# A list scheduler's price for matmuls, changed from one pair of constants to another

## The chip, the cores and the metric
One core of a Trainium2 chip. Its engines (TensorE for products, VectorE and ScalarE for elementwise work, SyncE for issuing transfers) each run their own queue of instructions in program order and wait for each other through semaphores. The metric is the device time of one execution, in microseconds.

## What is computed
A trunk of two layers over 256 latent tokens and 256 context tokens of width 1024. Each layer is: a SwiGLU sub-layer (width 2816), a mixer sub-layer, and a second SwiGLU sub-layer.

```
x = layer_norm(alpha*x + 0.5*gate * (silu(h@wg) * (h@wu)) @ wd)   # h = x*(1+scale)+shift
u,k,v,q,z,b,c,g = split(h @ w_in)
y_a = S5(u)           # two directions, state carried from context to latent
y_b = attention(q,k,v)   # 8 heads; latent: 4x64 neighbourhood + all context
y_c = b * conv3(c*z)
m   = sum_i sigmoid(g_i) * (y_i @ w_branch_i)
x   = layer_norm(alpha*x + gate * (m @ w_out))
x   = second SwiGLU sub-layer, as the first
```

Shift, scale and gate of every sub-layer come from products of a conditioning vector with `w_mod` (adaLN). In the last layer the context is needed only up to the mixer's keys, values and S5 states, so most work from there on has 256 columns in place of 512.

## The kernel before
Activations lie with features on the partitions and tokens along the free axis, in 8 tiles of 128 x 512 (context 0 to 255, latent 256 to 511). Every factor of a product is split into two parts of a rounded type (`hi`, and `lo` for what the rounding left out), and `mm3` issues three products, hi·hi, hi·lo and lo·hi, in place of one fp32 product. A few products of S5 and of the statistics are in plain fp32.

Weights come block by block (128 x 1024 fp32) through three raw buffers. ScalarE makes `whi` (`rounder`, L426), VectorE makes `wlo` (`remainder`, L453), both into a ring of three places, and TensorE gives a place back when a block's products are done (`release`, L485). A SwiGLU sub-layer takes 22 pairs of blocks `wg`, `wu` (`ffn`, L760), with 8 x 3 products each, and then the `wd` blocks (`residual`, L797), whose last tile goes stream by stream, so that one stream's LayerNorm (`normalize`, L647) can run under the other's products. `entry_products` (L737) are the next phase's first four products, feature tile by feature tile as they are normalized. The mixer (L1347) runs the S5 batches (L1147), attention units (`attend`, L1274) and the convolution beside its projections. Work that needs no activation runs beside it all: the dot products of adaLN on VectorE (`mod_chunks`, L519) and the S5 tables (`s5_tables`, L953).

The order of all this is not written out. Each line of work is a generator that names, ahead of each instruction, its engine and operands. The class `Plan` (L59) keeps a clock for each engine and a ready time for each tile. `run` (L106) takes the line whose next instruction can start first by these clocks; among those within 0.08 us it takes the one of better priority; `op` (L74) then books the instruction's cost:

```
end = max([self.t[eng], self.now] + [self.at(i) for i in ins]) + cost
self.ready[o.tensor.name] = end + self.LATENCY[eng]
```

The priorities (L222) run from statistics over LayerNorm, evacuation, the weight stream, attention, S5 and late work down to the main line of products (`P_MAIN`), which comes last. Room in the pools, banks of PSUM and places of the ring are counted in the same clock. VectorE's cost is 0.07 + columns/960 us (L284) and ScalarE's 0.09 + columns/1200, with additions for extra operands (L328). TensorE's is booked in `mm` (L349).

Of the kernel before, what the change touches and what calls it, by code (L numbers as in the profile page):

```python
# [9 lines left out]
F32R = mybir.dt.float32r  # L10
# [16 lines left out]
NORM_ACT = (True, False)  # L27
# the order of the mixers' heads, two by two, and channels of the convolution
ORDERS = ("h0 h1 c0 h2 c1 c2 h3 c3", "h0 h1 c0 h2 c1 c2 h3 c3")
# [8 lines left out]
N_SHIFT = 2  # L38
# whether the two parts of the values share a pass, by layer
SIDE = (True, False)  # L40
# [18 lines left out]
class Plan:  # L59
    """Engines run their instructions in program order. The lines of work are generators that say, ahead of each  # L60
    instruction, its engine and its operands (or what else they wait for); the one whose instruction can start first,
    by a rough count of the engines' time, puts it into that order."""

# [75 lines left out]
class Room:  # L139
    """a count of the tiles of a pool: lines of work wait until there is room for theirs"""  # L140

# [3 lines left out]
    def take(self, n, late=False):  # L145
        """what can come late leaves the kept part to the others"""
        def room():
            return self.n >= n + late * self.kept
        if not room():
            yield "WAIT", room  # L150
        self.n -= n
# [5 lines left out]
class Shift:  # L157
    """a tile that holds the columns of the later stream only"""

# [8 lines left out]
class Block:  # L168
    """a block of weights, split; for a product of k parts"""

# [4 lines left out]
def block_order():  # L175
# [10 lines left out]
    for l in range(DEPTH):  # L186
# [20 lines left out]
        ffn(l, 1)  # L207
    # the first blocks of a phase, which do not wait for the ring, come earlier than they are needed
    starts = [i for i, k in enumerate(order) if i and (k[0] == "wg" and k[3] == 0 or k[0] == "in" and k[2] == 0)]
# [10 lines left out]

# the order in which lines of work take an engine that several could have
P_STAT, P_CHAIN, P_ENTRY, P_NORM, P_EVAC, P_SOON, P_STREAM, P_ATT, P_S5, P_LATE, P_MAIN = range(11)  # L222


def _build(ctx, tc, nc, A):
# [50 lines left out]
    def pair(name, sl):  # L276
        """the two parts of a factor of the tensor engine: rounded, and what that left out"""
        if sl.start == 0:
            return slot(name + "hi", dt=F32R), slot(name + "lo", dt=F32R)
        t = slot(name, (128, 2, 256), F32R)  # L280
        return Shift(t[:, 0], 256), Shift(t[:, 1], 256)

# [1 line left out]
    def dve(o, ins, rate=1.0, extra=()):  # L284
# [64 lines left out]
    def mm(o, l, r, start, stop):  # L349
        PE.matmul(o, l, r, start=start, stop=stop)  # L350
        n = _free(r)
        P.op("PE", max(0.1077, n * 0.000421) if r.dtype == F32R else max(0.215, n * 0.00168), [o], (l, r))

# [20 lines left out]

# [1 line left out]
    order = block_order()  # L376
# [28 lines left out]
    def nth(key):  # L405
        """which of a phase's first blocks it is"""
        if key[0] in ("wg", "wu"):
            return 2 * key[3] + (key[0] == "wu")
        return key[2] if key[0] == "in" else len(order)

    def place(key):
        """where the two parts of a block go: a phase's first ones wait for its start beside the ring"""
        if key[0] in ("wg", "wu") and key[1:3] == (0, 0):
            return "slot" if nth(key) < N_FIRST else "ring"
        return "big" if nth(key) < 3 else "ring"
# [76 lines left out]

# [1 line left out]
    cT = const("cT", [128, KT, 2])  # L494
# [11 lines left out]

# [1 line left out]
    modt, vecs, gates = {}, {}, {}  # L508

    def mod_rows():  # L510
        """silu of the two conditioning vectors, on every partition"""
        rows = []
        for s in range(2):
            rows.append(big("crow"))
            yield from dma_(rows[s], A["crow"][s])
            yield from act_(rows[s], rows[s], AF.Silu)
        return rows
# [30 lines left out]
    def mod_vectors(l, i, sh, sc, lm, streams):  # L548
        """scale and shift of the modulated LayerNorm: t -> t*A + B"""
        yield from wait(lambda: (lm, sh) in modt and (lm, sc) in modt)  # L550
# [35 lines left out]

# [1 line left out]
    class Norm:  # L588
# [7 lines left out]
        def evac(self, m, ps, streams):  # L596
            """add a tile of the sub-layer's output"""
            key = (self.l, self.i)
# [16 lines left out]
        def shift(self):  # L615
            """a mean of the first tiles, so that the sums of squares stay near the variance"""
            sl = self.sl
# [29 lines left out]
        def normalize(self, s, done):  # L647
            """the statistics of a stream, token by token on the partitions, and back; then tile by tile"""
            yield from wait(lambda: self.late[s] == KT - N_SHIFT)
# [17 lines left out]
            give_bank(p)  # L667
            # minus the guarded variance; then Newton's steps for its root's inverse, each times a power of two
            for _, _, de, nv, *_ in groups:
# [67 lines left out]
    def entry_products(keys, streams):  # L737
        """the first four products of a phase, k by k as the modulated stream arrives"""
        pss = yield from bank_set("en", len(keys))
# [16 lines left out]

# [1 line left out]
    filled = [0]  # L758
# [38 lines left out]
    def residual(l, i, streams, key, cuts, src, n_tail, tail):  # L797
        """the products of a sub-layer's end, the sum with the residual and its LayerNorm; then the next phase's
        first products. The last blocks go stream by stream, so that one stream's LayerNorm runs under the other's"""
        sl = span(streams)  # L800
# [38 lines left out]

# [1 line left out]
    NS = 32 * DEPTH  # L841
# [9 lines left out]
    def cmul_(o0, o1, a0, a1, b0, b1, t, neg=False):  # L851
        """(o0, o1) = a*b, or its real part and minus its imaginary one"""
        yield from vtt_(o0, a0, b0, OP.mult)
        yield from vtt_(t, a1, b1, OP.mult)
        yield from vtt_(o0, o0, t, OP.subtract)
        yield from vtt_(o1, a0, b1, OP.mult)
        yield from vtt_(t, a1, b0, OP.mult)
        if neg:
            yield from stt_(o1, o1, -1.0, t, OP.mult, OP.subtract)
        else:  # L860
            yield from vtt_(o1, o1, t, OP.add)

    def s5_pre():
        """lam_bar, its phasor and decay over a chunk and the factor of b, per state"""
        yield from SL.take(4)
# [87 lines left out]
    def s5_tables(l):  # L953
        """what of S5 does not depend on its input, for the mixer to load: the powers of lam_bar over a chunk with b and
        with c, the kernel within a chunk, and the phasors"""
        yield from wait(lambda: l in SP)
# [65 lines left out]
    def rc_piece(rc, r, c):  # L1022
        """the readout of a state column: five powers of 32 channels"""
        n = 4 * r + c
        return rc[n // 3][:, 160 * (n % 3):160 * (n % 3) + 160]
# [88 lines left out]
    def s5(l, U, GH, G5, streams):  # L1114
        """the batches of two pairs of groups: states of the chunks, their scan in a rotating frame, readout"""
        sp = SP[l]
# [104 lines left out]
        def readout(b, M, rc, L):  # L1221
# [28 lines left out]
            g = YT[m].rearrange("p c i -> p (c i)")  # L1250
            # gelu as x sigmoid(2 sqrt(2 / pi) (x + 0.044715 x^3)), the same as its form with tanh
            yield from SL.take(1)
# [19 lines left out]

# [1 line left out]
    def attend(h, s, kq, Vt, y, bias, loading, next_bias, side):  # L1274
        """one head of one stream"""
        khi, klo, qhi, qlo = kq
# [52 lines left out]
        for kt in range(n):  # L1329
            hi, lo = pt[kt // 2]  # L1330
            v = Vt[kt][h // 4][:, h % 4]
            yield "PE", [hi, lo, v] + ([o] if kt == 0 else [])
            # side by side, the two parts of the values take one pass, and a sum when their product is copied
            if side:
# [10 lines left out]

# [1 line left out]
    def mixer(l, streams, N, ready, tail):  # L1347
# [25 lines left out]
        def chunks(m, ps):  # L1373
            """channels and the steps of a chunk on the partitions, chunks along the free axis"""
            yield from SL.take(1)
# [245 lines left out]

# [1 line left out]
    def first_products():  # L1623
        """the adaLN vectors of the first sub-layer, feature tile by feature tile, shared between the tensor engine
        and the vector engine, and the first products behind them"""
        mod0 = const("mod0_0", [128, KT, 2])
# [244 lines left out]
```

## Time and profile before

| | us |
|---|---|
| runs | 2198.79, 2201.69, 2203.39 |
| median | 2201.69 |
| profiled execution, span | 2202.1 |
| TensorE busy | 2151.3 (98%) |
| VectorE busy | 1669.5 (76%) |
| ScalarE busy | 1040.0 (47%) |
| DMA | 363.32 MB, mean 165 GB/s |

The page gives no other time of the profiled execution than its span. Busy time counts an engine as busy from an instruction's start to its end; products overlap, so the spacing of their starts, not the length of one, tells what a stream of them takes. The granted clock (PEclk) is the share of TensorE's full 2.4 GHz.

### The profile page before, as it was taken

Reading aid. Unit: us, or ns where it says so; the run is one execution under the profiler, and the core shown is the slowest. Engines: PE = TensorE matmul, PEld = TensorE weight load, DVE = VectorE, ACT = ScalarE, POOL = GpSimd, SP = SyncE. Lnnn points to the kernel's source line nnn. Section 1 sums busy time; section 2 is a strip of 40 time slices with the busy share of each in tenths; the row PEclk is TensorE's granted clock in tenths of the full one; section 3 lists DMA queues with packets and bytes.
Section 4 is the critical chain, followed back from the end, with each engine's and each line's share of the span. In section 5 each row is a group of like instructions: output and inputs, shape, how many; then the busy total and the mean of one; then the engine's idle time right before and its main releaser. Section 6 shows DMA issues by size and latency. Waiting matters only on the chain.

```text
span 2202.1 us, 32955 instructions
## 1 busy us (share of the span) xinstructions
PE 2151.3 (98%) x12090; PEld 1866.1 (85%) x12090; DVE 1669.5 (76%) x3987; ACT 1040.0 (47%) x1938; POOL 0.2 (0%) x4
## 2 busy tenths in 40 slices
PE   8999999999999999999999999999999999998997
PEld 5888888878888888988888898888888889998997
DVE  7799986887888856889838779973448988776555
ACT  5332225766654354632222585542226556555443
POOL 0000000000000000000000000000000000000000
PEclk9999999999999999999999999999999999998998
DMA  7666645353334333177624537862334544554553
GB/s 287 209 215 213 216 139 173 116 196 115 116 126 154 97 142 126 69 250 240 196 91 135 172 112 258 292 225 93 102 112 154 166 154 151 184 178 146 183 174 123
DMA packets 131970, 363.32 MB, mean 165 GB/s; under 512 B 15968, under 2 KB 41952, under 8 KB 131808
## 3 DMA queue, kind: packets, MB, share of 16 engines
q1 hardware_dynamic: 131808, 361.21, 48.8%
q8 instruction: 95, 1.56, 0.3%
q14 instruction: 67, 0.55, 0.1%
HBM read 331.79 MB, written 29.36 MB: 164 GB/s over the span
## 4 chain that ended last, share of the span: by engine, by line
PE 90%; DVE 5%; ACT 2%; DMA 1%; issue 1%; SPq 0%; ACTq 0%; DVEq 0%
PE psd L350 21%; PE pswu L350 17%; PE pswg L350 17%; PE pg L350 8%; PE en L350 7%; PE pbr L350 4%; PE pk L350 2%; PE pz L350 2%; PE Y L350 1%; PE pq L350 1%; PE pb L350 1%; PE pc L350 1%; PE sc L350 1%; PE pvv L350 1%; PE v L350 1%; DVE wlo L288 1%
## 5 line engine op out<-in xcount | busy, mean ns | idle before, releaser
L329 ACT ACTIVATE whi<-raw 128x1024 fp32r<-128x1024 f32 (+2 forms) x427 | 421.3, 988 | 885.1 <-issue 339.7
L288 DVE TENSOR_TENSOR wlo<-raw,whi 128x1024 fp32r<-128x1024 f32 (+2 forms) x427 | 483.3, 1133 | 285.7 <-ACT whi L329 278.2
L350 PE MATMUL psd<-ghi,whi 128*128 128x512 f32 (+1 forms) x594 | 221.8, 373 | 0.0
L350 PE MATMUL psd<-ghi,wlo 128*128 128x512 f32 (+1 forms) x594 | 217.4, 366 | 0.0
L350 PE MATMUL psd<-glo,whi 128*128 128x512 f32 (+1 forms) x594 | 217.3, 366 | 0.0
L350 PE MATMUL pswu<-hhi,whi 128*128 128x512 f32 x472 | 185.8, 394 | 0.0
L350 PE MATMUL pswg<-hhi,whi 128*128 128x512 f32 x472 | 185.2, 392 | 0.0
L350 PE MATMUL pswu<-hhi,wlo 128*128 128x512 f32 x472 | 183.9, 390 | 0.0
L350 PE MATMUL pswu<-hlo,whi 128*128 128x512 f32 x472 | 183.8, 389 | 0.0
L350 PE MATMUL pswg<-hhi,wlo 128*128 128x512 f32 x472 | 183.8, 389 | 0.0
L350 PE MATMUL pswg<-hlo,whi 128*128 128x512 f32 x472 | 183.8, 389 | 0.0
L296 DVE SCALAR_TENSOR_TENSOR mraw<-mraw,crow 128x1024 f32<-128x1024 f32 x128 | 155.8, 1222 | 4.6 <-DMA mraw<-wmod 3.1
L350 PE MATMUL pg<-hhi,whi 128*128 128x512 f32 (+1 forms) x384 | 130.2, 339 | 0.0
L350 PE MATMUL pg<-hhi,wlo 128*128 128x512 f32 (+1 forms) x384 | 129.2, 336 | 0.0
L350 PE MATMUL pg<-hlo,whi 128*128 128x512 f32 (+1 forms) x384 | 129.1, 336 | 0.0
L350 PEld LDWEIGHTS psd<-ghi,whi 128*128 128x128 f32 x594 | 112.1, 189 | 18.9
L350 PEld LDWEIGHTS psd<-ghi,wlo 128*128 128x128 f32 x594 | 111.9, 188 | 18.2
L350 PEld LDWEIGHTS psd<-glo,whi 128*128 128x128 f32 x594 | 112.1, 189 | 17.1
L296 DVE SCALAR_TENSOR_TENSOR mspare<-mraw,crow 128x1024 f32<-128x1024 f32 x96 | 117.1, 1220 | 0.0
L350 PEld LDWEIGHTS pswu<-hhi,whi 128*128 128x128 f32 x472 | 88.7, 188 | 18.9
L350 PEld LDWEIGHTS pswg<-hhi,whi 128*128 128x128 f32 x472 | 88.6, 188 | 19.0
L350 PEld LDWEIGHTS pswg<-hhi,wlo 128*128 128x128 f32 x472 | 88.7, 188 | 18.5
(348 smaller groups left out, 5014.2 us busy)
## 6 DMA issues: line engine op xcount, KB each, us to landing
mraw<-wmod SPq DMA_DIRECT2D x128, 512.0 KB, 4.3
raw<-win SPq DMA_DIRECT2D x96, 512.0 KB, 3.3
raw<-wg SPq DMA_DIRECT2D x88, 512.0 KB, 3.4
raw<-wu SPq DMA_DIRECT2D x88, 512.0 KB, 3.4
raw<-wd SPq DMA_DIRECT2D x64, 512.0 KB, 3.5
raw<-wd SPq DMA_DIRECT2D x32, 384.0 KB, 3.4
raw<-wbr SPq DMA_DIRECT2D x48, 256.0 KB, 2.7
mw<-wmod SPq DMA_DIRECT2D x32, 256.0 KB, 5.8
```

What stands on the lines that cost most here:

```text
L288: V.tensor_tensor(o, a, b, op=op)
L296: V.scalar_tensor_tensor(o, a, 1.0, b, op0=OP.mult, op1=OP.mult, accum_out=accum_out)
L329: S.activation(o, a, f, **k)
L350: PE.matmul(o, l, r, start=start, stop=stop)
```

## The change
The line of `mm` that books a product's cost gets other constants. For the rounded type it is now 0.0133 + 0.000417 us per column, at least 0.1115, where it was 0.000421 us per column, at least 0.1077. For fp32 it is twice 0.000844 us per column, at least twice 0.112, where it was 0.00168, at least 0.215. Nothing else of the code differs but comments and docstrings, which are left out. Transposes keep their cost of 0.108.

```
     def mm(o, l, r, start, stop):
         PE.matmul(o, l, r, start=start, stop=stop)
         n = _free(r)
-        P.op("PE", max(0.1077, n * 0.000421) if r.dtype == F32R else max(0.215, n * 0.00168), [o], (l, r))
+        one = max(0.1115, 0.0133 + n * 0.000417)
+        P.op("PE", one if r.dtype == F32R else 2 * max(0.112, n * 0.000844), [o], (l, r))
```

## Rows read from the trace of the kernel before

**Rows 1.** The page: busy time by engine; chain that ended last, by engine.
```profile
PE 2151.3 (98%) x12090; PEld 1866.1 (85%) x12090; DVE 1669.5 (76%) x3987; ACT 1040.0 (47%) x1938; POOL 0.2 (0%) x4
...
PE 90%; DVE 5%; ACT 2%; DMA 1%; issue 1%; SPq 0%; ACTq 0%; DVEq 0%
```

**Rows 2.** The chain in order of time: start us, duration us, what, instructions.
```profile
65.68 5.44 PE pswg L350 x24
...
266.96 5.44 PE pswu L350 x24
...
2123.09 17.28 PE psd L350 x144
```

**Rows 3.** Stretches: length, busy us (instructions) of each engine, clock, DMA.
```profile
core 0: us, PE busy (x) PEld busy (x) DVE busy (x) ACT busy (x) POOL busy (x), PEclk, DMA share, GB/s
0.00:65.70 65.70, 57.78 (x233) 37.14 (x234) 43.11 (x113) 33.64 (x60) 0.20 (x4) 0.95 0.79 285
65.70:272.40 206.70, 206.70 (x913) 171.25 (x913) 197.22 (x424) 60.55 (x75) 0.00 (x0) 1.00 0.63 213
272.40:432.50 160.10, 155.66 (x864) 135.61 (x864) 124.94 (x348) 85.00 (x179) 0.00 (x0) 0.98 0.41 132
432.50:857.50 425.00, 421.02 (x2143) 351.30 (x2143) 328.31 (x868) 232.27 (x498) 0.00 (x0) 1.00 0.40 136
857.50:932.20 74.70, 73.00 (x483) 67.33 (x483) 59.47 (x160) 42.62 (x77) 0.00 (x0) 0.98 0.26 93
932.20:1149.90 217.70, 217.70 (x962) 180.33 (x961) 168.96 (x254) 66.61 (x84) 0.00 (x0) 1.00 0.59 197
1149.90:1303.70 153.80, 152.50 (x853) 132.46 (x853) 123.28 (x380) 76.94 (x153) 0.00 (x0) 1.00 0.40 128
1303.70:1532.10 228.40, 228.40 (x1050) 188.22 (x1049) 166.83 (x332) 112.89 (x230) 0.00 (x0) 1.00 0.64 223
1532.10:1682.00 149.90, 148.71 (x814) 130.16 (x813) 76.90 (x176) 56.57 (x93) 0.00 (x0) 0.99 0.29 93
1682.00:1961.00 279.00, 269.01 (x2007) 253.48 (x2005) 235.11 (x666) 161.80 (x326) 0.00 (x0) 0.99 0.53 178
1961.00:2008.00 47.00, 39.83 (x284) 38.63 (x285) 35.83 (x95) 27.58 (x49) 0.00 (x0) 0.82 0.41 135
2008.00:2122.00 114.00, 114.00 (x953) 114.00 (x952) 64.01 (x81) 54.06 (x81) 0.00 (x0) 1.00 0.52 178
2122.00:2202.10 80.10, 67.00 (x552) 66.23 (x550) 45.54 (x97) 29.47 (x41) 0.00 (x0) 0.93 0.44 136
```

**Rows 4.** VectorE's waits, 65.7 to 272.4: total us, times, longest us.
```profile
DVE silu L288 <- PE en L350: 7.5, 1, 7.5
```

**Rows 5.** TensorE's waits over the whole span.
```profile
PE bc L355 <- DVE st L313: 6.3, 2, 3.1
PE pv L350 <- DVE ptlo L288: 5.9, 4, 3.4
```

**Rows 6.** Instructions in time order, crossing into the first mixer: start, duration.
```profile
401.22 0.38 PE L355 MATMUL bc<-ident,st 128*128 128x128 f32 x2
401.29 1.22 DVE L288 TENSOR_TENSOR wlo<-raw,whi 128x1024 fp32r<-128x1024 f32 x1
...
403.09 1.41 DVE L288 TENSOR_TENSOR ax<-ax,bc 128x256 f32<-128x256 f32 x4
...
405.65 0.58 PE L350 MATMUL en<-hhi,ehi 128*128 128x256 f32 x1 [1.59 <-ACT hhi L329]
```

**Rows 7.** Instructions in time order, second mixer: start, duration.
```profile
1794.02 0.60 PE L355 MATMUL pt<-ident,p 128*128 128x128 f32 x4
...
1796.22 2.00 ACT L329 ACTIVATE yT<-Y 32x64 f32<-32x64 f32 x7
...
1798.29 0.47 PE L350 MATMUL pv<-ptlo,v 128*64 128x256 f32 x1 [3.44 <-DVE ptlo L288]
```

## The prediction

> **What bounds the kernel now.** Read the busy shares and the chain first: TensorE is busy 2151.3 us of the 2202.1 us span and holds 90% of the chain that ended last, with VectorE at 5% and ScalarE at 2% [rows 1]. Then the chain in order of time, for the real spacing of matmuls: 24 products of 512 columns take 5.44 us, at 65.68 as at 266.96, so 226.7 ns each; 144 of 256 columns take 17.28 us, 120.0 ns each [rows 2]. Last the stretches, for where TensorE stands: span less busy time is 7.92 us in the start, 4.44 in the first sub-layer's end, 3.98 in the first mixer, 1.70, 1.30 and 1.19 in the next crossings, 9.99 in the second mixer, 7.17 in the crossing behind it and 13.10 at the end [rows 3]. In the four stretches of gate and up products it is 0.00 [rows 3].
>
> So no order can win more than what is idle or slow. The start waits for its first tiles, and the stretches 1961 to 2008 and 2122 to 2202 have one token stream, with nothing to put under its LayerNorm; their 28.2 us I hold fixed. What an order can reach is 4.44 + 3.98 + 1.70 + 1.30 + 1.19 + 9.99 = 22.6 us. Beside it stands the clock: the granted share is 0.98, 0.98, 0.99 and 0.99 in the stretches from 272.4, 857.5, 1532.1 and 1682 [rows 3]. With two levels, 2.4 and 1.2 GHz, a mean of c costs (1 - c) of the stretch: 3.2 + 1.5 + 1.5 + 2.8 = 9 us by these rounded figures. Ceiling of a gain: some 32 us, 1.4% of the time.
>
> **What the change does to the planner's count.** No instruction is added, removed or resized. Only the cost that the planner books for a product moves, and with it the order in which lines of work enter each engine's queue.
> - 512 columns, rounded type: 0.2156 before, 0.2268 after, against 226.7 ns measured [rows 2]: the old price is 4.9% short, the new one exact.
> - 256 columns: 0.1078 before, 0.1201 after, against 120.0 ns [rows 2]: 10.2% short, then exact.
> - 128 columns in plain fp32: 0.215 to 0.224, 256 columns 0.430 to 0.432. These pairs of passes are few, and 9 ns each moves nothing that can be seen in a stretch.
>
> Summed over a stretch: from 65.7 to 272.4 there are 38 blocks of 24 products. The old price books 38 x 24 x 0.2156 = 196.6 us, the new one 206.8 us, the trace shows 206.70 us, all of it busy [rows 3]. From 2008 to 2122, 953 products of 256 columns: 102.7 us, 114.4 us, and 114.00 in the trace [rows 3].
>
> The Trainium skill, page "TensorE: Matmul & The Clock Gate", section "Back-to-back issue gap", speaks against the change: it gives a warm spacing of columns / 2.4 plus 2.5 ns, which is an estimate of 215.8 ns for 512 columns and 109.2 for 256, nearly the old prices. The trace does not agree: 226.7 and 120.0 ns [rows 2]. By the rule the old planner was right and the new one books TensorE 5 to 10% too slow, the same fault as in the slower rival below and with its time.
>
> **Where that can move time, part by part.**
>
> *Gate and up products* (206.70 + 217.70 + 228.40 + 114.00 = 766.8 us [rows 3]). Their products run in program order and TensorE is never idle: no gain. A loss would need VectorE to fall behind with a split weight block. Between 65.7 and 272.4 VectorE is busy 197.22 us of 206.70 [rows 3], and 7.5 of its 9.5 idle us is one stand, for the first gate product [rows 4]. At the new price the planner sees 10.2 us more room in this stretch and fills it with the adaLN dot products and the S5 tables, which wait for nothing. VectorE would be near 100% busy; a split block has the time of two blocks, 10.9 us [rows 2], before TensorE needs it. Cost: 0, at most the 10.2 us of filling if that cover fails. What is filled here is gone from VectorE's 124.94 us of the next 160.10, and from the first mixer's 328.31 of 425.00 [rows 3]; with TensorE idle only 8.4 us in both, I book -1 us, between 0 and -8.4.
>
> *Crossings from sub-layer to sub-layer.* At 400 us the last products of the later stream (22 blocks x 3 = 66 of 256 columns) are booked 66 x 0.0123 = 0.8 us longer. What TensorE then waits for is a chain: the sums broadcast at 401.22, then VectorE takes a weight split of 1.22 us first, the tiles only at 403.09, and the first product of the next phase starts at 405.65 [rows 6]. The split goes first because it can start first; 0.8 us on the later stream's end does not give the tiles, whose broadcast comes after 401.29, an earlier place. So nothing is sure here. Best case: the split steps aside in each of the four crossings, 4 x 1.2 = -5 us, with less time at the low clock; worst case a split more gets ahead, +5. I take -0.5.
>
> *Mixers* (425.00 + 279.00 us [rows 3]). Here lines of work compete: S5 batches, attention units, and main products, which have the last priority and fill. Two effects pull against each other. (a) At the old price the planner believes that the second mixer has 10% less TensorE time under its 235.11 us of VectorE [rows 3], so it takes VectorE for nearly full and orders it too tightly; a right price gives it room. (b) The planner lets a product that depends on VectorE or ScalarE in at its first possible moment, without slack. The old price gave such a product a cushion: the filling ahead of it lasts 5% (512 columns) to 11% (256) longer than booked. The new price takes the cushion away, while other prices stay wrong. The S5 copies are booked at 0.09 + 64/1200 = 0.143 us; seven of them take 2.00 us, 0.286 each [rows 7]. There are 64 in the second mixer: 64 x 0.143 = 9.2 us of ScalarE that the planner does not see. That this delay reaches TensorE is seen at 1794: transposes at 1794.02, seven copies at 1796.22, the value product held 3.44 us until 1798.29 [rows 7]. Of TensorE's waits, 5.9 us in 4 are of this form [rows 5].
> Bounds: (a) at best half of the mixers' idle 3.98 + 9.99 and of the 2.8 us of low clock, -8 us; (b) at worst the 9.2 us whole, plus a second visit to the low clock as dear as the 2.8 of now, +12. Both are near their rows only in part; I take -1 for (a) and +1 for (b).
>
> Sum: 0 - 1 - 0.5 - 1 + 1 = -1.5 us. The profiled execution (2202.1 us of span, which the page gives without a further time around it) lies 0.4 us above the median of 2201.69, so the sum is set on the median: 2200 us.
>
> **Rivals.**
> - *Faster by over 0.2%.* The right price lets the planner spread VectorE work better, in the stretch of 65.7 and in the second mixer. For: VectorE there is 95% and 84% busy [rows 3], and the longest waits of TensorE end on VectorE or ScalarE, as bc on st, 6.3 us in 2 [rows 5]. Against: those 6.3 are two chains of 3.1 us, as in the one-stream LayerNorms, which no order shortens. Time: -1 - 5 x 0.6 - 8 x 0.8 = -10, so 2191 us.
> - *Slower: the cushion is gone.* Place: the mixers, above all 1682 to 1961; price: up to 12 us as in (b); it decides from the point where ScalarE's unseen 2.3 us per S5 tile (16 copies x 0.143) is more than the filling ahead of the tile's dependent products holds back. At the old price some 20 us of filling held 2.3 us back. For: the 3.44 us wait has this form already [rows 7]. Against: in the first mixer, where the cushion was only 5%, TensorE idles 3.98 of 425 us [rows 3]. Time: +12 less the 1 + 0.5 of the other parts, some 2212 us.
> - *The order hardly changes.* For: 35% of the time runs in program order whatever the price. Against: lines that can start within 0.08 us of each other change places easily, and 0.8 us per 66 products is ten times that. Time: 2201.7 us.
> - *TensorE's price was right*, as the page's rule has it: the slower rival's time, 2212, against both spacings of [rows 2].
>
> **Numbers.** What the measurement tells from no change is about 0.2%, 4.4 us: 2197.3 to 2206.1. Forecast of a small net move within it, 0.36; order nearly unchanged, 0.04; faster 0.33; slower 0.25; old price right, 0.02. So faster 0.33, same 0.40, slower 0.27. The likeliest case's own range is 2197 to 2206. To leave out no more than 2 in 10, the range goes to 2186 (a gain of half the ceiling of 32) and to 2215 (the slower rival with one further low-clock visit of 3 us): 2186 to 2215.
>
> **What would show it.** Right: no idle TensorE in the four stretches of gate and up products, the same 226.7 and 120.0 ns, VectorE over 97% busy in the first of them, and fewer VectorE and ScalarE waits for the products. TensorE's waits on ptlo, p and M grow if (b) holds and shrink if (a) does; a further stretch at the 1.2 GHz level in a mixer would be (b) at its dearest. Wrong: idle TensorE in the first stretch (VectorE over-filled), or the one-stream stretches of 47 and 80 us moved by over 2 us, which I hold fixed.

## The result and the profile after

The changed kernel takes 2228.8 us (median of 4 runs, 2227.36 to 2232.67) against 2200.64 for the kernel before: ratio 1.013, 95% interval 1.0116 to 1.0144. It is slower by 1.3%, outside the range of 2186 to 2215. The profiled execution after has a span of 2225.74 us, 23.6 above that of before, so the two traces hold most of the 28 us between the medians.

The page after, parts 1 and 4. The rows of before are [rows 1].

```profile
PE 2164.4 (97%) x12090; PEld 1869.8 (84%) x12090; DVE 1665.6 (75%) x3987; ACT 1038.3 (47%) x1938; POOL 0.2 (0%) x4
...
PE 82%; DVE 9%; ACT 5%; DMA 2%; issue 2%; SPq 0%; ACTq 0%; DVEq 0%
```

The same 12090 products, and 82% of the last chain on TensorE where it was 90%: more of the chain runs through VectorE (9%, was 5%) and ScalarE (5%, was 2%).

To compare stretches they must hold the same products. So both traces were cut again at the first product of each kind: the first `pswg`, `psd`, then (after both mixers) the first output product, and so on. Busy time by stretch of the kernel before, cut that way (length, then busy us and instructions of TensorE, its weight loads, VectorE, ScalarE and GpSimd, then clock, DMA share, GB/s):

```profile
0.00:65.52 65.52, 57.60 (x233) 36.96 (x233) 43.11 (x113) 33.64 (x60) 0.20 (x4) 0.95 0.80 285
65.52:272.24 206.72, 206.72 (x914) 171.27 (x912) 197.06 (x424) 60.55 (x75) 0.00 (x0) 1.00 0.63 212
272.24:857.32 585.08, 576.66 (x3005) 486.90 (x3004) 453.42 (x1216) 317.11 (x675) 0.00 (x0) 0.99 0.40 135
857.32:932.09 74.77, 73.07 (x484) 67.39 (x482) 59.36 (x160) 42.67 (x77) 0.00 (x0) 0.98 0.26 92
...
1149.72:1303.54 153.82, 152.52 (x853) 132.48 (x852) 123.12 (x380) 76.96 (x153) 0.00 (x0) 1.00 0.40 128
1303.54:1531.95 228.41, 228.41 (x1050) 188.24 (x1049) 166.99 (x332) 112.90 (x230) 0.00 (x0) 1.00 0.64 223
1531.95:1681.90 149.95, 148.76 (x813) 130.20 (x812) 76.80 (x176) 56.62 (x93) 0.00 (x0) 0.99 0.29 93
1681.90:1956.41 274.51, 266.26 (x1987) 250.93 (x1985) 232.11 (x662) 160.41 (x324) 0.00 (x0) 0.99 0.53 178
1956.41:2007.73 51.32, 42.42 (x305) 41.02 (x303) 38.92 (x98) 28.80 (x51) 0.00 (x0) 0.83 0.42 141
2007.73:2122.93 115.20, 115.20 (x963) 115.20 (x962) 64.50 (x81) 54.33 (x82) 0.00 (x0) 1.00 0.52 178
2122.93:2202.12 79.19, 66.07 (x544) 65.30 (x542) 45.04 (x96) 29.47 (x41) 0.00 (x0) 0.93 0.44 135
```

And of the kernel after:

```profile
0.00:65.73 65.73, 57.10 (x232) 36.82 (x233) 42.82 (x113) 33.53 (x60) 0.20 (x4) 0.95 0.79 285
65.73:272.45 206.72, 206.72 (x913) 171.17 (x912) 202.88 (x450) 61.06 (x76) 0.00 (x0) 1.00 0.67 212
272.45:862.51 590.06, 582.83 (x3005) 487.73 (x3004) 445.07 (x1190) 319.61 (x677) 0.00 (x0) 0.99 0.41 134
862.51:938.62 76.11, 73.28 (x483) 67.40 (x482) 59.38 (x160) 42.57 (x77) 0.00 (x0) 0.98 0.28 91
...
1156.25:1311.17 154.92, 152.77 (x854) 132.33 (x852) 124.47 (x384) 78.89 (x163) 0.00 (x0) 1.00 0.42 129
1311.17:1544.08 232.91, 229.43 (x1051) 187.85 (x1050) 165.83 (x327) 110.22 (x220) 0.00 (x0) 1.00 0.64 218
1544.08:1692.78 148.70, 147.77 (x813) 128.63 (x812) 76.50 (x176) 56.15 (x93) 0.00 (x0) 1.00 0.31 93
1692.78:1981.79 289.01, 275.40 (x1986) 258.62 (x1985) 233.19 (x662) 156.93 (x322) 0.00 (x0) 0.96 0.52 169
1981.79:2031.35 49.56, 40.16 (x304) 38.57 (x303) 38.73 (x98) 28.98 (x51) 0.00 (x0) 0.90 0.44 145
2031.35:2146.55 115.20, 115.20 (x962) 115.20 (x961) 64.50 (x81) 54.39 (x82) 0.00 (x0) 1.00 0.55 178
2146.55:2225.74 79.19, 66.07 (x544) 65.30 (x542) 45.02 (x96) 29.45 (x41) 0.00 (x0) 0.92 0.46 135
```

The lengths differ by 0.2 in the start, 5.0 in the first crossing with the first mixer, 1.3, 1.1, 4.5 in the second layer's first gate and up products, -1.3, 14.5 in the second mixer, -1.8, and nothing elsewhere: 23.6 in all. Most is the second mixer, 274.51 to 289.01 us. There TensorE's idle time (length less busy) goes from 8.25 to 13.61 us, +5.4, and its busy time for the same products from 266.26 to 275.40, +9.1. The second figure is nearly all the clock: granted 0.96 in place of 0.99. At two levels a mean of 0.96 costs 289 x 0.04 = 11.6 us and 0.99 costs 2.7. The clock records of the two traces agree: before, one stretch at 1.2 GHz in this mixer, 6.8 us from 1797.9, with the wait of 3.4 us; after, five stretches, 23.9 us together, from 1748.9, 1766.0, 1820.6, 1858.1 and 1953.7. Each of the five starts within 2 us behind a wait: of 1.3 us, of 1.9 and 0.7, of 1.8, of 2.8, and of 0.7 and 0.9. Half of each is lost: 3.4 us before, 11.9 after, 8.5 more. So the waits cost more by the clock that falls behind them than by themselves.

In the first mixer's stretch the loss does not show as idle time: that falls from 8.42 to 7.23 us, while the busy time of the same 3005 products rises by 6.2, at the same 6.8 us of low clock. That points to waits too short to reach beyond the modelled end of a product.

TensorE's longest waits in the second mixer, before (total us, times, longest us; under 1 us more is left out):

```profile
PE pv L350 <- DVE ptlo L288: 5.6, 3, 3.4
PE pt L355 <- ACT p L329: 1.8, 1, 1.8
```

And after (1.9 us more, of branch products and one weight block, is left out):

```profile
PE pv L350 <- DVE ptlo L288: 4.8, 4, 1.9
PE pt L356 <- ACT p L329: 3.3, 2, 2.8
PE pt L356 <- DVE p L313: 2.3, 2, 1.7
PE sc L350 <- ACT q L329: 1.3, 1, 1.3
```

They became more in number and kind, and these are all of attention's products on what VectorE and ScalarE make for them. The longest, in order of time (start, duration):

```profile
1850.81 2.02 ACT L329 ACTIVATE yT<-Y 32x64 f32<-32x64 f32 x7
...
1853.18 1.04 ACT L329 ACTIVATE whi<-raw 128x1024 fp32r<-128x1024 f32 x1
1854.26 1.23 DVE L288 TENSOR_TENSOR wlo<-raw,whi 128x1024 fp32r<-128x1024 f32 x1 [1.09 <-ACT whi L329]
...
1855.60 0.14 DVE L325 RECIPROCAL pw<-pw 128x2 f32<-128x2 f32 x1
...
1855.78 0.72 ACT L329 ACTIVATE p<-p,pw 128x512 f32<-128x512 f32 x1 [1.55 <-DVE pw L325]
...
1856.55 0.66 PE L356 MATMUL pt<-ident,p 128*128 128x128 f32 x4 [2.82 <-ACT p L329]
```

Seven S5 copies stand ahead of a weight block's `whi`, VectorE stands still for that `whi` with its `wlo`, the reciprocal of the softmax stands behind the `wlo`, ScalarE's scaling behind the reciprocal, and the transposes on TensorE behind that. It is the form of [rows 7]. No engine is full; each waits in its order for another.

### The profile page after: what moved, and what is told of

The parts are those of the page before. It is cut to its first block, busy times and chain, and to the rows that moved or that the text cites. A ratio compares the mean times of both kernels' runs of the same rounds, so it can differ in the third digit from the quotient of the medians.

```text
span 2225.7 us, 32979 instructions
## 1 busy us (share of the span) xinstructions
PE 2164.4 (97%) x12090; PEld 1869.8 (84%) x12090; DVE 1665.6 (75%) x3987; ACT 1038.3 (47%) x1938; POOL 0.2 (0%) x4
## 4 chain that ended last, share of the span: by engine, by line
PE 82%; DVE 9%; ACT 5%; DMA 2%; issue 2%; SPq 0%; ACTq 0%; DVEq 0%
PE psd L350 19%; PE pswu L350 16%; PE pswg L350 16%; PE pg L350 7%; PE en L350 4%; PE pbr L350 4%; PE pvv L350 2%; DVE wlo L288 2%; PE pk L350 2%; PE Y L350 1%; PE pz L350 1%; ACT yT L329 1%; PE pb L350 1%; PE pq L350 1%; ACT whi L329 1%
## 5 line engine op out<-in xcount | busy, mean ns | idle before, releaser
L350 PEld LDWEIGHTS pswu<-hhi,wlo 128*128 128x128 f32 x472 | 88.7, 188 | 18.5
```

## The experiments

Each edit is made to the kernel before or after, as named. Times stand beside a run of the kernel before on the same chip. "First mixer" is the stretch from the first `psd` of layer 0 to its first output product, "gate/up" the second layer's first gate and up products, "second mixer" from the first `pvv` of layer 1 to its first output product; each holds the same products in every run (those of the S5 tables apart, which are few). Times are single executions, as are their kernels before, but for after (4 runs, 4 of before), mix1_short (4) and exact_to_mixer0 (11, both with 17 of before). Those 17 lie between 2198.92 and 2204.38 us and the 4 of mix1_short between 2206.46 and 2214.28, so a single time is good to a few us. Stretches come from one profiled execution each.

| run | time us | before | first mixer | gate/up | second mixer |
|---|---|---|---|---|---|
| before | | 2200.64 | 585.08 | 228.41 | 274.51 |
| after | 2228.80 | 2200.64 | 590.06 | 232.91 | 289.01 |
| old_nudge | 2206.99 | 2202.83 | 589.80 | 230.78 | 274.93 |
| new_nudge | 2223.64 | 2202.83 | 589.73 | 230.55 | 285.28 |
| only_512 | 2216.01 | 2202.83 | 591.86 | 235.35 | 273.66 |
| only_256 | 2208.17 | 2202.83 | 585.07 | 230.94 | 280.28 |
| dose_97 | 2226.58 | 2202.83 | 600.32 | 228.62 | 283.86 |
| dose_90 | 2237.32 | 2202.83 | 613.89 | 226.50 | 279.78 |
| after_lat | 2249.04 | 2202.83 | 606.52 | 229.45 | 273.45 |
| after_fit | 2215.23 | 2202.83 | 580.61 | 230.08 | 286.04 |
| mix_only | 2222.88 | 2201.22 | 592.58 | 228.46 | 289.87 |
| mix_old | 2218.09 | 2201.22 | 589.36 | 234.95 | 273.77 |
| mix1_only | 2213.33 | 2201.22 | 584.69 | 228.38 | 287.96 |
| before_fit | 2213.73 | 2201.22 | 594.27 | 228.48 | 277.53 |
| after_att | 2225.49 | 2199.52 | 587.91 | 234.86 | 283.31 |
| before_att | 2216.71 | 2199.52 | 592.76 | 228.38 | 283.61 |
| after_att_late | 2220.89 | 2199.52 | 591.25 | 231.64 | 282.26 |
| before_att_late | 2241.85 | 2199.52 | 607.27 | 228.53 | 284.86 |
| mix1_short | 2210.97 | 2201.44 | 584.33 | 228.38 | 282.39 |
| exact_to_mixer0 | 2199.58 | 2201.44 | 580.45 | 229.04 | 276.37 |

### How much is mere chance: old_nudge, new_nudge

```
+ old_nudge:  P.op("PE", 1.001 * (old price), ...)
+ new_nudge:  P.op("PE", 1.001 * (new price), ...)
```

> The kernel before with its matmul prices times 1.001 (0.2158 us for 512 columns), still short of the measured spacing. Cushion theory (a short price holds dependent products back, so they wait less): 0.1% of cushion is nothing, 2196 to 2206 us, lost TensorE time in the two mixers' projection stretches within 4 us of the kernel before. Chance theory (the order is so sensitive that any new price draws another order, and the order of before was a lucky one): the order changes in many places all the same, and the time goes up by 8 us or more, to 2209 to 2235 us.

> The changed kernel with its matmul prices times 1.001. Cushion theory: as the changed kernel, 2222 to 2236 us, since 0.1% of cushion brings nothing back. Chance theory: another draw, anywhere between 2195 and 2240 us; a time below 2212 us speaks for it.

Measured 4 us above and 5 us below their parents; old_nudge is just above the cushion theory's range and below the chance theory's. A price changed by a thousandth moves the time by as much, so no single difference under some 5 us may be read as an effect of the price. The chance theory in its strong form (any new order costs 8 us or more) did not come out; in the weak form it did: of the 5.0 us that the first mixer's stretch lost by the change, old_nudge loses 4.7, where runs with the order of before repeat 585.08 within 0.8 (mix1_short 584.33, mix1_only 584.69).

The second mixer is another matter: 274.93 for the one, 285.28 for the other. But there the nudges do not test chance. Compared tile name by tile name in the traces, the 1984 named products of the second mixer stand in old_nudge in the very order of before, and in new_nudge in that of after but for three products. The nudges repeat two orders there and draw no new one. The row in old_nudge:

```profile
1687.67:1962.60 274.93, 266.46 (x1986) 250.71 (x1985) 232.01 (x662) 160.37 (x324) 0.00 (x0) 0.99 0.54 177
```

and in new_nudge:

```profile
1691.71:1976.99 285.28, 272.08 (x1987) 255.55 (x1985) 233.13 (x662) 156.39 (x322) 0.00 (x0) 0.97 0.53 171
```

### Which of the prices: only_512, only_256

```
+ only_512:  one = 0.0133 + n * 0.000417 if n > 256 else max(0.1077, n * 0.000421)
+ only_256:  one = max(0.1115, 0.0133 + n * 0.000417) if n <= 256 else n * 0.000421
```

> The new price for 512 columns alone (0.2268 us); 256 columns and plain fp32 keep the old ones. Cushion theory: the first mixer (512 columns) loses its cushion and costs about 7 us more as in the changed kernel, the second mixer (256 columns) keeps it: 2206 to 2214 us, with the second mixer's projection stretch losing about 10 us as before, not 23. Chance theory: no such split by stage; the second mixer's loss may be anywhere from 8 to 25 us, since its order changes with everything ahead of it.

> The new price for 256 columns alone (0.1201 us); 512 columns keep the old one. Cushion theory: the second mixer loses its cushion, 13 us more lost in its projection stretch (23 us in place of 10), the first mixer as before (6.5 us lost): 2212 to 2222 us. Chance theory: no split by stage, anything from 2195 to 2235 us.

The second mixer, whose products have 256 columns but for keys and values, stays at 273.66 with the price of 512 columns alone and goes to 280.28 with that of 256 alone, about 6 of the 14.5 us. The first mixer, with 512 columns, loses 6.8 us by the one and nothing by the other, and the gate and up products 6.9 and 2.5. The split by stretch that the cushion theory asked for is there, though less than its numbers in the second mixer. The totals missed its ranges, 2216.01 us above 2206 to 2214 and 2208.17 below 2212 to 2222, and the first mixer's 6.8 is little more than the nudge's 4.7.

### The size of the price: dose_97, dose_90

```
+ P.op("PE", 0.97 * (new price), ...)      # and 0.90
```

> All new matmul prices times 0.97 (512 columns 0.2200 us, 256 columns 0.1165, 3% short). Cushion theory: part of the loss comes back, 2209 to 2219 us, with lost TensorE time in the mixers' two projection stretches between the 16.5 us of before and the 37 us of after. Chance theory: no order by size, 2200 to 2235 us.

> All new matmul prices times 0.90 (512 columns 0.2041 us, 256 columns 0.1080; as short for 256 columns as before, 5% shorter for 512). Cushion theory: no slower than before, 2192 to 2206 us, with the first mixer and the second layer's gate and up products losing no more than before (6.5 and 1.0 us). Chance theory: 2200 to 2235 us; over 2212 us speaks for it.

Both missed what the cushion theory expected, and lie where the chance theory had put them or above. With prices 3% short the time is that of the changed kernel, with 10% short 2237 us. In dose_90 most of the loss lies in the first mixer, 613.89 us, where the price of 512 columns is 10% short in place of 5%. The stretch, and TensorE's longest waits over the whole span of dose_90:

```profile
272.45:886.34 613.89, 588.02 (x3006) 490.40 (x3005) 465.72 (x1243) 320.09 (x677) 0.00 (x0) 0.98 0.41 130
```

```profile
PE glu L350 <- ACT gghi L329: 10.3, 1, 10.3
PE pt L356 <- ACT p L329: 8.5, 4, 7.1
```

In the first mixer the gate products of S5 stand 10.3 us for an S5 tile. The wait of 7.1 us for an attention unit's `p` is in the second mixer, which takes 279.78 us at a price of 256 columns within 0.3% of the old one. That too much held back is as bad as too little, because the last S5 batch and the last heads come late, is a reading of these waits; after_lat below, which holds back in another way, has the same wait of 10.3 us. No run separates it from a bad order by chance.

### Slack without a short price, and right prices for the other engines: after_lat, after_fit

```
after_lat:
- LATENCY = {"PE": 0.2, "DVE": 0.13, "ACT": 0.13, "DMA": 2.0}
+ LATENCY = {"PE": 0.2, "DVE": 0.45, "ACT": 0.45, "DMA": 2.0}
after_fit, in act(), scan() and vcopy():
+ yT copies 0.18 + n * 0.00172; U copies 0.28 (ScalarE), 0.299 (VectorE); L copies 0.427
+ scans 0.26; 1.29 more where the function table changes (Exp, Silu, Sigmoid)
```

> The changed kernel with the planner's booked latency of a VectorE or ScalarE result at 0.45 us in place of 0.13: the matmul price stays exact, but a dependent product is held back by 0.32 us per step. Cushion theory: it is the slack that matters and not the price, so this brings back a good part, 2202 to 2216 us, TensorE's waits on ptlo, p and vtb under 8 us (15 in the changed kernel). Chance theory: another draw around the changed kernel's 2224, with no reason to be below 2212.

> The changed kernel with the worst ScalarE and VectorE prices set to the measured spacing too: yT copies 0.29 us (64 columns) and 0.40 (128), U copies 0.28 and 0.30, L copies 0.43, scans 0.26, and 1.29 us at each change of ScalarE's function table. Theory that the loss is the mismatch of a right matmul price with short prices of the other engines: the second mixer's lost time falls from 28 to under 18 us, total 2200 to 2214 us. Cushion theory, that slack itself is needed because the rest of the timing is uncertain: a smaller gain, 2212 to 2224 us. Chance theory: 2200 to 2235 us.

after_lat is the worst of all in total, 33 us above the cushion theory's range, and as good as the best in the second mixer: 273.45 us, at the exact matmul price. TensorE's longest waits there:

```profile
PE pbr L350 <- DVE bp L288: 2.0, 3, 0.9
PE glu L350 <- ACT gg L329: 1.3, 1, 1.3
PE pvv L350 <- DVE wlo L288: 1.3, 1, 1.3
PE pt L356 <- ACT p L329: 1.2, 1, 1.2
```

The wait on `ptlo` is gone and that on `p` is 1.2 us. So slack booked as latency takes these waits away. It was paid for elsewhere: the stretches just ahead of this mixer and just behind it are 7.1 and 3.5 us longer than before (157.03 and 54.85), and over the span the broadcast of the LayerNorm waits 18.6 us for its statistics, and the S5 gate products 10.3 us.

after_fit refutes the copies as the cause of most of the loss. With their prices right the second mixer still takes 286.04 us at 0.96 of the clock, 3 us less than after; the waits move from the copies' victims to others (`pt` on `p` 7.6 us by both engines). What it gained, 13 us against the changed kernel, lies mostly in the first mixer, 580.61.

```profile
273.27:853.88 580.61, 576.50 (x3005) 486.02 (x3004) 446.48 (x1190) 323.16 (x679) 0.00 (x0) 1.00 0.42 136
...
1681.98:1968.02 286.04, 271.99 (x1987) 255.58 (x1985) 233.87 (x662) 157.87 (x322) 0.00 (x0) 0.96 0.52 170
```

### Where the price acts: mix_only, mix_old, mix1_only; and before_fit

```
+ mixing = [None]       # the mixer sets it to its layer, and to None ahead of the output products
+ mix_only:   new price if mixing[0] is not None, else old
+ mix_old:    new price if mixing[0] is None, else old
+ mix1_only:  new price if mixing[0] == 1, else old
  before_fit: the kernel before with the ScalarE and VectorE prices of after_fit
```

> New matmul prices only while the main line is between a mixer's first and last projection, old ones everywhere else. Theory that the loss arises inside the mixers, where lines of work compete: 2214 to 2228 us, the two projection stretches losing over 28 us together (16.5 before, 37 after). Theory that what the price does ahead of a mixer (fuller VectorE, later tables) sets it: 2198 to 2210 us. Chance theory: anything from 2198 to 2235.

> The complement: new matmul prices everywhere but between a mixer's first and last projection. Mixer theory: 2200 to 2210 us, projection stretches losing 12 to 21 us together. Theory of what is ahead: 2214 to 2228 us. Chance theory: the mixers' order differs too, because what enters them does, so anything from 2198 to 2235.

> New matmul prices in the second mixer alone; the order ahead of it is that of the kernel before. If the exact price by itself makes this mixer worse (cushion), its projection and branch stretches lose 22 to 30 us (13.7 before, 28 after), total 2210 to 2218 us. If the loss hangs on the order that enters it (chance), they may lose 9 to 30 us; under 17 us speaks against the cushion.

> The kernel before, old matmul prices kept, with the corrected ScalarE and VectorE prices of after_fit. Theory of matched prices (a short matmul price goes well with short prices of the other engines): correcting the others alone unbalances it the other way, 2206 to 2220 us. Theory that any price nearer to the trace helps: 2190 to 2200 us. Chance theory (the order of before is a lucky draw among many): 2205 to 2230 us.

This settles which price carries the second mixer's loss: the one booked inside it. With the new price inside it, it takes 289.87 (mix_only) and 287.96 us (mix1_only, where the order ahead of it is that of the kernel before); with the old price inside and the new one ahead of it 273.77 (mix_old). The traces show what the price does: mix_only and mix1_only have, product for product, the order of after in this mixer, mix_old (and exact_to_mixer0 below) that of before. Its row in mix1_only, and then in mix_old:

```profile
1680.61:1968.57 287.96, 273.87 (x1986) 257.03 (x1985) 233.01 (x662) 156.80 (x322) 0.00 (x0) 0.96 0.52 169
```

```profile
1697.27:1971.04 273.77, 264.96 (x1987) 249.93 (x1986) 231.84 (x662) 160.67 (x324) 0.00 (x0) 0.99 0.55 178
```

So these runs repeat the two orders, of before and of after, and cannot tell an exact price from one unlucky order. Other runs have other orders there. At the old price of 256 columns, or within 0.3% of it, they take 273.66 (only_512), 277.53 (before_fit) and 279.78 us (dose_90); at the new one 280.28 (only_256) and 286.04 (after_fit). With before's 274.51 and after's 289.01 that makes four orders at the short price, all below the three at the exact one, if narrowly. The direction is borne out; of the size, 14.5 us, a good part can be the luck of two orders.

By its total mix_old missed: 2218.09 us, where the mixer theory had 2200 to 2210 and the rival, that the price acts ahead of the mixers, 2214 to 2228. Outside the mixers the new price costs some 17 us by itself, and the two halves, 21.7 and 16.9, add up to more than the whole 28: it is not the second mixer alone.

The first mixer does not divide so: 589.36 at the old price with another order entering, 592.58 at the new price with the old order entering, 594.27 with the old matmul price and the others right. These three cost it 4 to 9 us, and the nudge 4.7. By its total before_fit, 2213.73 us, lies in the ranges of matched prices and of chance, and well above the 2190 to 2200 that were to show that any truer price helps. And the gate and up products lose where the new price is booked outside the mixers (234.95) and not where it is booked in them (228.46).

### Slack for chosen lines: after_att, before_att, after_att_late, before_att_late

```
+ slack = 0.32 if eng in ("ACT", "DVE") and self.current.prio in (P_ATT,) else 0.0   # or (P_ATT, P_LATE)
- self.ready[o.tensor.name] = end + self.LATENCY[eng]
+ self.ready[o.tensor.name] = end + self.LATENCY[eng] + slack
```

> The changed kernel with 0.32 us more booked latency for VectorE and ScalarE results of attention lines alone. Slack theory: the second mixer's projection and branch stretches lose 10 to 16 us together in place of 28, TensorE's waits on p and ptlo fall from 12.5 us to under 6, total 2205 to 2216 us. If the price acts in another way: 22 to 30 us lost there, total 2217 to 2230.

> The kernel before, old price, with the same 0.32 us for attention lines. Slack theory, if the old price did not give enough of it: the second mixer's 13.7 us fall to 5 to 10, total 2192 to 2199 us; if it gave enough, 2200 to 2210 (held back for nothing). Chance theory for the first mixer: its 7.8 us may be anything from 5 to 20.

> after_att with the slack for late lines (S5 tables, adaLN) too. Slack theory: TensorE's waits on vtb in the second layer's gate and up products, 3.3 us of the 5.5 lost there, fall under 1 us, total 2 to 5 us below after_att. Against it: the tables' transposes come later and wait elsewhere, total as after_att or above.

> before_att with the slack for late lines too. At the old price the vtp waits are under 1 us already, so slack theory expects nothing from the late lines: within 4 us of before_att, apart from what the order of the tables does in the first mixer (chance, up to 10 us either way).

after_att missed what slack theory expected: the second mixer comes down from 289.01 to 283.31 us only. Waits on `p` fall to 1.8 us, those on `ptlo` stay at 5.3. A likely reason, not shown by a run of its own: attention's results are held up by other lines' work in VectorE's and ScalarE's queues, as in the chain above, and slack for attention alone does not move that work. For late lines the expectation was near: after_att_late is 4.6 us below after_att, and its gate and up products lose 3.2 us less, though the waits on `vtb` there only fall from 3.7 to 2.1 us and 4.6 us is no more than a nudge is worth. At the old price both totals missed every range that was put down: the same slack costs 17 us (before_att: `pt` on `p` 12.5 us in the second mixer) and 42 us.

### Both sides of the old price, and the best stretches joined: mix1_short, exact_to_mixer0

```
+ mix1_short:       0.95 * (old price) if mixing[0] == 1, else old
+ exact_to_mixer0:  all prices as after_fit up to the first mixer's last branch product, all old from there
```

> The kernel before with its matmul prices 5% shorter still in the second mixer alone (256 columns 0.1024 us, 15% short); the order ahead of it is that of the kernel before. Cushion theory alone: its projection and branch stretches lose as little as before or less, 8 to 14 us, total 2195 to 2203. Two-sided theory (too much cushion makes attention and S5 end late): they lose 16 to 25 us, total 2205 to 2214.

> Exact prices of all three engines (as after_fit) up to the end of the first mixer's branches, the old prices from there on. If the loss of the second mixer comes from the price booked inside it: the first mixer loses 6 us as in after_fit, the second 12 to 16 as with the old price, total 2193 to 2199 us, faster than both kernels. If it hangs on the whole order: second mixer 14 to 28 us, total 2200 to 2215.

mix1_short: ratio 1.005, interval 1.0036 to 1.0065, so 0.5% slower than before, as the two-sided theory said. With the same order entering, the second mixer takes 282.39 us at a price of 256 columns of 0.1024, 274.51 at 0.1078 and 287.96 at 0.1201. Here the old price lies between two losses; but each of the three prices is seen through one order, and dose_97, at 0.1165, takes 283.86 us and not a time between the last two. The row in mix1_short:

```profile
1679.85:1962.24 282.39, 270.06 (x1986) 253.33 (x1985) 231.79 (x662) 159.84 (x324) 0.00 (x0) 0.98 0.53 173
```

exact_to_mixer0: 2199.58 against 2201.44 us, ratio 0.9989, interval 0.998 to 0.9998, the only version here that beats both kernels, by 0.1%, just outside the expected 2193 to 2199. Its first mixer is that of after_fit (580.45), its second has the order of before (276.37). Against before the one gives 4.6 us and the other takes 1.9; the whole trace is 3.5 us shorter. That is less than a nudge moves, so the gain is one order's and not shown to be the exact price's. Its rows for the two:

```profile
272.79:853.24 580.45, 576.36 (x3005) 485.88 (x3004) 446.50 (x1190) 323.11 (x679) 0.00 (x0) 1.00 0.43 136
...
1680.10:1956.47 276.37, 267.76 (x1986) 251.85 (x1985) 231.93 (x662) 160.62 (x324) 0.00 (x0) 0.98 0.54 177
```

## Why the prediction was wrong, point by point

- **What bounds the kernel, and the price itself**: right. The 960 products of 256 columns in the last gate and up stretch take 115.20 us, 120.0 ns each, before and after. The Trainium skill's rule of columns / 2.4 plus 2.5 ns (page "TensorE: Matmul & The Clock Gate", section "Back-to-back issue gap") again disagrees with that; by it 256 columns would take an estimated 109.2 ns. The prediction left out that this section gives the rule for an isolated product and about 131 ns at 512 columns for a stream of products with their weight loads, which the 226.7 ns of [rows 2] do not bear out either. The new price is the true one, and the kernel planned with it is slower.
- **Gate and up products, no gain, no loss**: right for three of the four, and VectorE was filled as forecast in the first, 202.88 us in place of 197.06 of 206.72, at no cost. Wrong for the second layer's, +4.5 us: I took TensorE never to wait there. But the S5 tables' transposes go to TensorE in that stretch too, and 3.3 us in 3 waits are theirs for `vtb`; before there are none:

```profile
PE vtp L356 <- ACT vtb L329: 3.3, 3, 2.0
```

old_nudge, at the old price, loses 2.4 us there with one such wait of 2.1 us, so about half of the 4.5 can be scatter of the order.
- **Crossings, -0.5 us between -5 and +5**: the crossings behind the first mixer give 1.3, 1.1, -1.3 and -1.8 us. Right. The first crossing and the first mixer together lose 5.0, where -1 was booked; as old_nudge loses 4.7 there, that cannot be told from the scatter of the order.
- **Mixers: "I take -1 for (a) and +1 for (b)"**: this is the step that failed. (a), that a right price gives room, is not to be seen: VectorE's busy time in the second mixer is 232 us before and 233 after and TensorE waits more. (b), booked at +1, measured 14.5 us in the second mixer, the largest part of the 23.6 against a forecast sum of -1.5. Its bound of 12 was too low by its clock term: 5.4 us of waits was below the 9.2 allowed, but the clock cost 8.5 us more in place of a second 2.8. The sign that I had named for (b) at its dearest, a further stretch at 1.2 GHz in a mixer, came four times over; of the waits that were to grow with it, over the whole span, those on `p` did (2.9 to 7.2 us) and those on `ptlo` and `M` did not (5.9 to 5.3, 2.1 to 2.4). I had both ends on the page and took a value near zero because two unknown effects had opposite signs; that is no reason to let them cancel.
- **The rival "the cushion is gone"** had the right place and sign; its 2212 us is less than half of the way from 2200 to 2228.8. Its reason, 2.3 us of unseen copies per S5 tile, was wrong for most of it: after_fit prices them and all but 3 us of the loss stays. What the runs show is this: the price booked inside the second mixer sets the order there, and the order that the exact price gave makes TensorE wait more, in four executions of it (one, new_nudge, with three products moved; 285.28 to 289.87 us against 273.77 to 276.37 in four of the old one). What they do not show is the cushion, that the old price kept dependent products back by the right amount. For it speak the four orders against three, and that slack booked as latency brings the stretch to 273.45. Against it, from the end of a `ptlo` to the products that read it pass 2.1 us in the mean of the second mixer before and 2.5 after, and 1.4 in only_512, whose second mixer is as short as any. That the old order was in part a lucky one stays open.
- **The chance of faster, 0.33**, rested on room for VectorE. No price that was tried for the whole kernel came out faster; 0.1% was to be had only by exact prices up to the first mixer and the short one behind it.

Open: why just the first mixer gains from exact prices of all engines (580.5 us, in two runs of one order) and not from any other set; one order cannot tell a cause from luck, when a nudge of a thousandth is worth 4.7 us there. Open too is whether the second mixer needs slack or only a luckier order; slack for attention alone did not bring it back. Several orders at each price of the second mixer, drawn for instance by small changes of the priorities or of NEAR (the 0.08 us), would tell.

## What to carry to other kernels

A list scheduler that starts each instruction at its first possible moment leaves no slack, and engines that run in program order pay for each late operand; a price that is short may stand in for the slack, which the runs here make likely and do not prove. A truer price is no surer way to a better order. Before the constants of such a planner are corrected, nudge one by a thousandth to see how far mere reordering moves the time, and look in the trace whether the nudge did reorder the stretch in question: here it did in the first mixer and not in the second. Then try the correction stretch by stretch. And a wait in the middle of dense products is to be priced with the clock that falls behind it, not only with its own length.

## What was not expected of the hardware

Behind waits of 0.7 to 2.8 us within the second mixer TensorE's clock fell to 1.2 GHz five times in place of once, 23.9 us in place of 6.8, and the same products were busy 275.40 us in place of 266.26, at a mean granted clock of 0.96 in place of 0.99. Not every wait does it: before, those of 1.3 us at 1746.1 and of 1.8 us at 1844.0 were followed by no fall. The clock's share of that stretch's loss, 8.5 us, was larger than the waits' own, 5.4.
